# The out projection of a streaming encoder block as 2x2x2 block products by seven products instead of eight

## The chip, the cores and the metric

The kernel runs on one core of a Trainium2 chip. The metric is the device time in microseconds of one execution. Three runs of the kernel before gave 970.71, 971.36 and 972.44 us; the median is 971.36.

## The reference

One encoder layer on 512 tokens (and 16 meta tokens in front), model width 1024, all in fp32. The change concerns `merged @ w_out`; the lines after it are what waits for its result.

```python
xn = rmsnorm(h, norm_mix_g[l])
proj = xn @ w_in[l]
...
y_sb = o_sb @ w_br_sb[l]
y_df = o_df @ w_br_df[l]
gates = jax.nn.sigmoid(xn @ w_gate[l] + b_gate[l]).reshape(B, L_pad, 2, D)
merged = gates[:, :, 0] * y_sb + gates[:, :, 1] * y_df
h = h + merged @ w_out[l]
hn = rmsnorm(h, norm_ffn_g[l])
h = h + (jax.nn.silu(hn @ w_ffn_gate[l]) * (hn @ w_ffn_up[l])) @ w_ffn_down[l]
```

`o_sb` comes from a stick-breaking attention of 8 heads, `o_df` from a differential attention of 8 heads.

## The kernel before

Every matmul is made in three passes (`mm3`, L262 to L264): each operand is split into a rounded high part and the rest (`split`, L76: ScalarE casts the high part, L77; VectorE subtracts it, L78), and high x high, high x low and low x high are summed in PSUM. So everything that TensorE reads, weights too, passes once through ScalarE and VectorE.

The work runs in stages: input projection and the stick-breaking heads, the differential heads, the gate stage, the out projection, the FFN's gate and up projections, the down projection. Activations lie transposed in the gate stage (`mg_h`, `mg_l`: model row by token), so that in the out projection a token tile of 128 is the stationary operand and 512 output columns stream.

**Weights.** All of them form one list, `stream`. `stage_one` (L157) issues the DMA of the next one on SP (L179) into one of three `wst` buffers of 512 KB; `prepare` casts it into one of four `wh`/`wl` pairs. `weights(key)` asks for a chunk and prepares `READY` = 3 (after the first part of the kernel 2) chunks beyond it. A cast can only start when an earlier chunk's pair has been read for the last time.

**Background jobs.** The down projection is already made with seven products instead of eight. Its weight sums are made in DRAM by 48 DMAs on POOL's queue (`sum_job`, L136 to L141): copies of a block, and accumulating ones that read a block and add it to a sum (`ds` in the profile). During the heads one job is put in for every two units of projection work (L993 to L995). Each job waits for the last cast that was written before it, which paces it.

**Gate stage (L1028 to L1038).** For each of the eight 128-row blocks f, both branches' outputs come back from DRAM (`y_back`, `y_part`; stored on POOL's queue at L766 and L768, `y_df<-y_out`), two gates are computed (24 matmuls of 128x512 each; f = 0 and 1 already in the heads' stage), POOL multiplies each gate with its branch (L1036), VectorE adds the two (L1037), and `split` cuts the sum into `mg_h[:, f]`, `mg_l[:, f]`. The residual input `hres` is then loaded by four DMAs on POOL's queue (L1044); the tile takes the place of `y_out`.

**Out projection (`accumulate`, L1047).** Two column halves, each over 8 k and 4 token tiles; half 0 accumulates in the two `z` tiles, half 1 in four `mm` tiles with its last six k token tile by token tile, so that tiles end one after the other. After each tile: VectorE adds the bank into `hres` (L1068), ScalarE squares it with a row sum (L1071), and `done(t)` calls `normed(t)` (rstd, then `hn`, L1092). After tile 2, `turned(0)` transposes tiles 0 and 1 on TensorE (L1101, 16 transposes) and cuts them into `hT_h` (ScalarE, L1106) and `hT_l` (VectorE, L1107). The first FFN products on tokens 0 to 255 follow, then tile 3, `turned(1)`, and `block_sums` (L1113 to L1125), which makes the token sums t1 to t4 that the FFN's seven products need.

The scheduler places instructions on each engine by priorities; each engine then runs its own list in order.

Of the kernel before, what the change touches and what calls it, by code (L numbers as in the profile page):

```python
# [40 lines left out]
def block_kernel(ctx: ExitStack, tc: tile.TileContext, x, meta, norm_mix_g, w_in, w_gate, b_gate,  # L41
# [94 lines left out]
    def sum_job(to, of, k0, add):  # L136
        src = raw_down(of, k0) if of in raw_at else w_sum[of, k0][:, 0:min(2, NK - k0)]
        dst = w_sum[to, k0][:, 0:min(2, NK - k0)]
        kw = dict(accum_op=ALU.add, max_dma_last_dim=2048) if add else {}
        paced = mybir.DependencyInfo(mybir.DependencyClass.Sync, mybir.DependencyReason.DATA)  # L140
        tc.add_manual_dep(nc.gpsimd.dma_start(dst, src, **kw).ins, cast["last"].ins.name, paced)  # L141

    background = [(to, of, k0, i > 3) for i, (to, of) in enumerate(
        (("s1", "a21"), ("s2", "a11"), ("s3", "a21"), ("s4", "a12"), ("s1", "a22"), ("s3", "a11"), ("s2", "s1"), ("s4", "s2")))
        for k0 in DK]
# [880 lines left out]

    ys = [y_back(f) for f in range(2)]
    for f in range(KT):  # L1028
# [3 lines left out]
        for br, y in enumerate(ys[f]):  # L1032
            if f > 1:
                for u in gate(br, f, sg[br], AF.Sigmoid):
                    u()
            nc.gpsimd.tensor_tensor(sg[br], sg[br], y, op=ALU.mult)  # L1036
        nc.vector.tensor_tensor(sg[0], sg[0], sg[1], op=ALU.add)  # L1037
# [9 lines left out]
    def accumulate(pool, name, act, nk, half, tail, done, banks):  # L1047

        if banks == "z":
            zt = [z_tile() for _ in range(2)]  # L1050
            acc = [zt[t // 2][:, t % 2] for t in range(NQ)]
        else:
            acc = [mm_tile() for _ in range(NQ)]

        def step(k, t):
            ah, al = act(half, k)
            wh, wl = weights((name, half, k // 2 * 2))
            q = slice(t * P, (t + 1) * P)
            mm3(acc[t], [(ah[:, q], al[:, q], wh[:, k % 2], wl[:, k % 2])], k == 0, k == nk - 1)

        cs = slice(half * 512, (half + 1) * 512)
        for k in range(nk - tail):
            for t in range(NQ):
                step(k, t)
        for t in range(NQ):
            for k in range(nk - tail, nk):
                step(k, t)
            nc.vector.tensor_tensor(hres[:, t, cs], hres[:, t, cs], acc[t], op=ALU.add)  # L1068
            sq = pool.tile([P, 512], F32, tag="y_sb", bufs=2, name="sq")
# [350 lines left out]
```

## Time and profile before

| | |
|---|---|
| median of 3 runs | 971.36 us |
| the profiled execution | 970.92 us |
| its span | 969.1 us |
| PE busy | 948.4 us |
| VectorE, ScalarE, POOL busy | 701.2, 588.0, 183.8 us |
| gate stage | 505 to 579 us of the span |
| out projection | 578.92 to 624.44 us |
| entry to the FFN | 625 to 660 us |

The profile shows one execution; times in it are microseconds from the span's start. PE is TensorE's matmuls, DVE VectorE, ACT ScalarE, POOL GpSimd, SPq and POOLq the queues that issue DMAs. A row of a timeline has the start, the length, the engine, the line of the kernel and `out<-in`, and in brackets how long the engine had been idle and what released it. Buffer numbers are left out of names: `z` and `mm` are PSUM tiles, `wst` a staged weight, `wh` and `wl` its two parts, `sg` a gate tile, `ds` the weight sums in DRAM. Matmuls are pipelined, so their lengths overlap; the distance of their starts is what one costs.

### The profile page before, as it was taken

To read this page: it belongs to the slowest core of one execution; us is meant where nothing else is said; L and a number is where in the kernel's file an instruction comes from. 1 tells how busy PE (TensorE), PEld (TensorE's weight loads), DVE (VectorE), ACT (ScalarE), POOL (GpSimd) and SP (SyncE) were. 2 spreads that over 40 slices of the span, in tenths; PEclk is the share of its full clock that TensorE was granted. 3 is DMA by queue.
4 is the path that set the end of the run, shared out by engine and by line. 5 is a ranking of instruction groups with operands and counts; after the bars stand their busy time and mean duration, and the time that the engine had idled before them with its cause. 6 is when DMAs were issued, how large, how long until landed. Compare 5 with 4: busy or idle time off the path is not lost.

```text
span 969.1 us, 16156 instructions
## 1 busy us (share of the span) xinstructions
PE 948.4 (98%) x6117; PEld 853.8 (88%) x6118; DVE 701.2 (72%) x1292; ACT 588.0 (61%) x1128; POOL 183.8 (19%) x198
## 2 busy tenths in 40 slices
PE   8998999999999999999999999989999999999997
PEld 6997888898899998999878888879999999988886
DVE  7988687766567776678632433699888888989785
ACT  7666766666566666666773433575555555666554
POOL 3201111222353433422315430000000000000013
PEclk9999999999999999999999999999999999999999
DMA  8334656679989989754739733124433334276552
GB/s 242 109 104 126 188 167 176 171 164 208 194 183 189 172 199 198 155 139 111 153 100 259 237 121 100 57 62 134 129 89 111 108 95 123 67 240 205 181 168 87
DMA packets 151439, 145.83 MB, mean 150 GB/s; under 512 B 6049, under 2 KB 116802, under 8 KB 151362
## 3 DMA queue, kind: packets, MB, share of 16 engines
q1 hardware_dynamic: 131794, 97.94, 34.0%
q0 software_dynamic: 19408, 46.80, 23.8%
q8 instruction: 48, 0.79, 0.3%
q14 instruction: 29, 0.24, 0.1%
q10 hardware_dynamic: 160, 0.07, 0.0%
HBM read 121.59 MB, written 41.94 MB: 169 GB/s over the span
## 4 chain that ended last, share of the span: by engine, by line
PE 86%; DVE 6%; ACT 4%; DMA 3%; issue 1%; DVEq 0%; ACTq 0%; SPq 0%
PE mm L264 19%; PE mm L263 19%; PE mm L262 19%; PE z L262 7%; PE z L263 7%; PE z L264 7%; DMA wst<-in_w_in_dram 2%; PE z L673 1%; PE z L672 1%; DVE wl L78 1%; PE tr L528 1%; PE z L528 1%; ACT wh L77 1%; PE tr L504 1%; PE z L556 0%
## 5 line engine op out<-in xcount | busy, mean ns | idle before, releaser
L262 PE MATMUL mm<-xT_h,wh 128*128 128x264 f32 (+2 forms) x656 | 214.3, 327 | 0.5 <-ACT xT_h L865 0.5
L78 DVE TENSOR_TENSOR wl<-wst,wh 128x1024 fp32r<-128x1024 f32 (+1 forms) x146 | 162.3, 1116 | 72.1 <-ACT wh L77 72.0
L263 PE MATMUL mm<-xT_l,wh 128*128 128x264 f32 (+2 forms) x656 | 213.2, 325 | 0.5
L264 PE MATMUL mm<-xT_h,wl 128*128 128x264 f32 (+2 forms) x656 | 212.8, 324 | 0.0
L77 ACT CAST wh<-wst 128x1024 fp32r<-128x1024 f32 (+1 forms) x146 | 140.2, 962 | 103.0 <-PE mm L263 70.0
L263 PEld LDWEIGHTS mm<-xT_l,wh 128*128 128x128 f32 x656 | 123.4, 188 | 10.4 <-DVE xT_l L866 1.3
L262 PEld LDWEIGHTS mm<-xT_h,wh 128*128 128x128 f32 x656 | 123.6, 188 | 10.0 <-ACT xT_h L865 0.9
L264 PEld LDWEIGHTS mm<-xT_h,wl 128*128 128x128 f32 x656 | 123.4, 188 | 9.9
L263 PE MATMUL mm<-hT_l,wh 128*128 128x256 f32 x284 | 80.6, 285 | 0.7 <-DVE hT_l L1107 0.7
L262 PE MATMUL mm<-hT_h,wh 128*128 128x256 f32 x284 | 80.3, 285 | 0.6 <-DVE sg L1202 0.6
L264 PE MATMUL mm<-hT_h,wl 128*128 128x256 f32 x284 | 80.1, 283 | 0.0
L1322 POOL TENSOR_TENSOR outs<-hres,gF 128x512 f32<-128x512 f32 x4 | 7.2, 1799 | 283.2 <-DVE hres L1308 278.1
L141 POOL DMA_DIRECT2D ds<-in_w_ffn_down_dram x36 | 28.5, 791 | 156.0 <-ACT wh L77 106.0
L676 DVE CUSTOM_DVE_ANT_0 pr<-z,bias 128x144 f32<-128x144 f32 (+3 forms) x64 | 30.9, 502 | 35.0 <-PE z L673 34.9
L263 PEld LDWEIGHTS mm<-hT_l,wh 128*128 128x128 f32 x284 | 53.7, 189 | 1.1 <-DVE hT_l L1107 1.1
L262 PEld LDWEIGHTS mm<-hT_h,wh 128*128 128x128 f32 x284 | 53.4, 189 | 1.0 <-DVE sg L1202 0.8
L264 PEld LDWEIGHTS mm<-hT_h,wl 128*128 128x128 f32 x284 | 53.6, 189 | 0.0
L262 PE MATMUL mm<-o_h,wh 128*128 128x512 f32 x128 | 53.1, 415 | 0.0
L262 PE MATMUL z<-wh,da 128*128 128x512 f32 (+1 forms) x132 | 50.9, 386 | 0.3 <-DVE hres L1308 0.3
L264 PE MATMUL mm<-o_h,wl 128*128 128x512 f32 x128 | 50.8, 397 | 0.0
L263 PE MATMUL mm<-o_l,wh 128*128 128x512 f32 x128 | 50.1, 392 | 0.3 <-DVE o_l L744 0.3
L263 PE MATMUL z<-wl,da 128*128 128x512 f32 (+1 forms) x132 | 50.4, 382 | 0.0
(344 smaller groups left out, 2560.1 us busy)
## 6 DMA issues: line engine op xcount, KB each, us to landing
wst<-in_w_in_dram SPq DMA_DIRECT2D x40, 512.0 KB, 7.2
ds<-in_w_ffn_down_dram POOLq DMA_DIRECT2D x30, 512.0 KB, 5.1
wst<-in_w_ffn_gate_dram SPq DMA_DIRECT2D x22, 512.0 KB, 3.8
wsu<-in_w_ffn_up_dram SPq DMA_DIRECT2D x21, 512.0 KB, 3.8
y_df<-y_out POOLq DMA_DIRECT2D x32, 256.0 KB, 5.7
wst<-in_w_gate_dram SPq DMA_DIRECT2D x16, 512.0 KB, 5.9
slots<-ds SPq DMA_DIRECT2D x13, 512.0 KB, 3.3
ds<-ds POOLq DMA_DIRECT2D x10, 512.0 KB, 8.1
```

The costliest lines, as they stand in the source:

```text
L77: cast["last"] = (hi_copy or nc.scalar.copy)(hi, src)
L78: (lo_eng or nc.vector).tensor_tensor(lo, src, hi.bitcast(F32), op=ALU.subtract)
L141: tc.add_manual_dep(nc.gpsimd.dma_start(dst, src, **kw).ins, cast["last"].ins.name, paced)
L262: nc.tensor.matmul(ps, lhsT=ah, rhs=bh, start=(start and i == 0), stop=False, skip_group_check=skip)
L263: nc.tensor.matmul(ps, lhsT=ah, rhs=bl, start=False, stop=False, skip_group_check=skip)
L264: nc.tensor.matmul(ps, lhsT=al, rhs=bh, start=False, stop=(stop and i == n - 1), skip_group_check=skip)
L504: nc.tensor.transpose(pt[:, j * P:(j + 1) * P], vT[:, j * P:(j + 1) * P], ident)
L528: nc.tensor.transpose(pt[:, (t - j) * P:(t - j + 1) * P], blocks(t, j * P, (j + 1) * P), ident)
L672: nc.tensor.matmul(o, lhsT=q[c][:, qs], rhs=k[c][:, 0, k0:k1], start=True, stop=False)
L673: nc.tensor.matmul(o, lhsT=q[c][:, qs], rhs=k[c][:, 1, k0:k1], start=False, stop=True)
L676: nc.vector.tensor_tensor_reduce(po, zz, bb, scale=1.0, scalar=-3.0e38, op0=ALU.add, op1=ALU.max, accum_out=mx[:, t, c:c + 1])
L1322: nc.gpsimd.tensor_tensor(outs[t][:, D1], hres[:, t, D1], gF[:, D1], op=ALU.mult)
```

## The change

`merged` (512 x 1024) and `w_out` (1024 x 1024) are each taken as 2x2 blocks. The product is made with seven block products instead of eight, each of 256 tokens x 512 k x 512 columns, two token tiles and 4 k each:

- The list `OUT` names them: weight operand, token operand, PSUM accumulator. Three accumulators, `acc[0]` to `acc[2]`, each of two banks, are added into `hres` (`to_out`) as soon as a product that completes a term is done: 14 adds of 128x512 instead of 8.
- The weight sums s1 to s4 are made in DRAM by 16 more background jobs, 8 copies and 8 accumulating ones, of two 128x512 blocks each. They stand ahead of the 48 jobs of the down projection. `tick` replaces the count of units; it is also called in the gate stage after each gate unit, and twice per step of the FFN loop.
- The out projection reads 14 weight chunks of 512 KB instead of 8 (six raw, eight sums). Two of every five of them are loaded into the upper half of a new tile `mf` (`oslots`) instead of a `wst` buffer; `READY` is 3 for them.
- The token sums t1 to t4 are made in the gate loop (`merge_sums`). For f below 4 the merged row stays in `mf`; t1 is cut from it. For f from 4 on, t2, t3 and t4 are made of rows f and f - 4. `b12`, the row block that no product uses alone, is not cut; t3 takes its place in `mg_h` and `mg_l`.
- Token tiles 0 and 1 are complete after the fifth product; tiles 2 and 3 after the sixth and seventh, which are made for tile 2 first and then for tile 3.

The diff, cut to its core:

```diff
+    o_sum = {(n, k0): sums_dram.tile([P, 2, 512], F32, name=f"o{n}_{k0}") for n in ("s1", "s2", "s3", "s4") for k0 in (0, 2)}
+    OUT = (("a11", "b11", 0), ("s1", "t1", 2), ("s2", "t2", 0), ("s4", "b22", 2), ("s3", "t3", 0), ("a12", "b21", 1),
+           ("a22", "t4", 0))
...
+    def sum_jobs(raw, kept, ks):
+        return [lambda to=to, of=of, k0=k0, i=i: summed_in(kept(to, k0), (raw if of[0] == "a" else kept)(of, k0), i > 3)
+                for i, (to, of) in enumerate((("s1", "a21"), ("s2", "a11"), ("s3", "a21"), ("s4", "a12"),
+                                              ("s1", "a22"), ("s3", "a11"), ("s2", "s1"), ("s4", "s2")))
+                for k0 in ks]
...
+    background = sum_jobs(raw_out, lambda w, k0: o_sum[w, k0], (0, 2)) + sum_jobs(raw_down, lambda w, k0: w_sum[w, k0][:, 0:min(2, NK - k0)], DK)
+    ticks = [0]
+
+    def tick(num=1, den=2):
+        ticks[0] += 1
+        if background and ticks[0] * num // den > (ticks[0] - 1) * num // den:
+            background.pop(0)()
...
-            slot = (n - first_down) % 7 - 3 if n >= first_down else -1
-            if slot < 0:
+            slot = (n - first_down) % 7 - 3 if n >= first_down else (n - first_out) % 5 - 3 if key[0] == "out" else -1
+            if key[0] == "out" and slot >= 0:
+                st = fpools["oslots"][:, slot]
+            elif slot < 0:
...
+    def merge_sums(f, m):
+        k = f % 4
+        b11, b12 = mf[:, k, T2], mf[:, k, T1]
+        if f < 4:
+            split(mg_h[:, f, T2], mg_l[:, f, T2], b11)
+            nc.vector.tensor_tensor(b11, b11, b12, op=sub)
+            split(*(v[:, k] for v in tsum["t1"]), b11)
+        else:
+            b21, b22 = m[:, T2], m[:, T1]
+            nc.vector.tensor_tensor(b11, b11, b22, op=add)
+            cut(tsum["t2"], k, b11, -1.0)
+            split(mg_h[:, f], mg_l[:, f], m)
+            nc.vector.tensor_tensor(b12, b22, b12, op=sub)
+            split(mg_h[:, k, T1], mg_l[:, k, T1], b12)
+            nc.vector.tensor_tensor(b21, b11, b21, op=sub)
+            split(*(v[:, k] for v in tsum["t4"]), b21)
...
                 for u in gate(br, f, sg[br], AF.Sigmoid):
                     u()
+                    tick()
             nc.gpsimd.tensor_tensor(sg[br], sg[br], y, op=ALU.mult)
-        nc.vector.tensor_tensor(sg[0], sg[0], sg[1], op=ALU.add)
-        split(mg_h[:, f], mg_l[:, f], sg[0])
+        m = mf[:, f] if f < 4 else sg[0]
+        nc.vector.tensor_tensor(m, sg[0], sg[1], op=ALU.add)
+        merge_sums(f, m)
...
-    accumulate(mgp, "out", merged, KT, 0, 0, lambda t: None, "z")
-    accumulate(mgp, "out", merged, KT, 1, 6, done, "mm")
...
+    def out_steps(i, t):
+        w, b, e = OUT[i]
+        ah, al = otok[b]
+        q = slice(t * P, (t + 1) * P)
+        for k in range(4):
+            wh, wl = weights(("out", w, k // 2 * 2))
+            mm3(acc[e][t], [(ah[:, k, q], al[:, k, q], wh[:, k % 2], wl[:, k % 2])],
+                k == 0 and w in ("a11", "s1", "a12"), k == 3, True)
...
+    for t in range(2):
+        out_steps(5, t)
+        to_out(2 + t, 0, acc[1][t], add, True)
+        out_steps(6, t)
+        to_out(2 + t, 1, acc[0][t], sub, True)
```

The scheduler puts the changed program into another order on each engine. Three places matter below.

POOL in the gate stage, before. `y_df<-y_out` are the stores of the differential branch's rows, `sg<-sg,y_sb` and `sg<-sg,y_df` the products of a gate with its branch.

```order
158 L1036 TENSOR_TENSOR sg<-sg,y_sb 128x512 x2
159 L768 DMA y_df_115<-y_out 128x512
160 L768 DMA y_df_116<-y_out 128x512
161 L768 DMA y_df_117<-y_out 128x512
162 L768 DMA y_df_118<-y_out 128x512
163 L1036 TENSOR_TENSOR sg<-sg,y_df 128x512
164 L768 DMA y_df_119<-y_out 128x512
165 L1036 TENSOR_TENSOR sg<-sg,y_df 128x512
166 L768 DMA y_df_120<-y_out 128x512
167 L768 DMA y_df_121<-y_out 128x512
168 L1044 DMA hres<-in_x_dram 128x1024 x2
169 L1036 TENSOR_TENSOR sg<-sg,y_sb 128x512
```

And now, from row 2's store on (`ds<-ds` are accumulating jobs):

```order
172 L791 DMA y_df_124<-y_out 128x512
173 L143 DMA ds_2_103<-ds_2_91 256x512
174 L791 DMA y_df_125<-y_out 128x512
177 L791 DMA y_df_128<-y_out 128x512
178 L1089 TENSOR_TENSOR sg<-sg,y_df 128x512 x2
179 L143 DMA ds_4_104<-ds_4_92 256x512
180 L791 DMA y_df_129<-y_out 128x512
181 L1098 DMA hres<-in_x_dram 128x1024
182 L1089 TENSOR_TENSOR sg<-sg,y_sb 128x512
183 L143 DMA ds_6_105<-ds_6_93 256x512
185 L143 DMA ds_8_106<-ds_8_94 256x512
186 L1089 TENSOR_TENSOR sg<-sg,y_df 128x512
```

(Rows 175, 176 and 184, two more stores and two `hres` loads, are left out.) Jobs of the down projection's sums now stand between the stores, ahead of the last store (`y_df_129`, row 7), and between the products of row 2. Before, none stood here.

TensorE where the out projection ends, before. `z<-ident,hn` are the transposes of `turned(0)`:

```order
3588 L262 MATMUL mm<-wh,mg_h 128x512
3589 L1101 MATMUL z<-ident,hn 128x128 x4
3590 L263 MATMUL mm<-wl,mg_h 128x512
3591 L264 MATMUL mm<-wh,mg_l 128x512
3592 L262 MATMUL mm<-wh,mg_h 128x512
3593 L263 MATMUL mm<-wl,mg_h 128x512
3594 L264 MATMUL mm<-wh,mg_l 128x512
3595 L1101 MATMUL z<-ident,hn 128x128 x4
3596 L262 MATMUL mm<-wh,mg_h 128x512
3597 L263 MATMUL mm<-wl,mg_h 128x512
3598 L264 MATMUL mm<-wh,mg_l 128x512
3599 L262 MATMUL mm<-hT_h,wh 128x256
```

And now, after the last matmul of the out projection and five of the FFN:

```order
3579 L287 MATMUL mm<-hT_h,wl 128x256
3580 L285 MATMUL mm<-hT_h,wh 128x256 x2
3581 L286 MATMUL mm<-hT_l,wh 128x256
3582 L285 MATMUL mm<-hT_h,wh 128x256
3583 L286 MATMUL mm<-hT_l,wh 128x256
3584 L1124 MATMUL z<-ident,hn 128x128 x4
3585 L286 MATMUL mm<-hT_l,wh 128x256
3586 L1124 MATMUL z<-ident,hn 128x128 x4
3587 L287 MATMUL mm<-hT_h,wl 128x256
3588 L286 MATMUL mm<-hT_l,wh 128x256
```

The last eight transposes of `turned(0)` have moved from before the end of the out projection to behind the first twelve matmuls of the FFN.

VectorE at the same place, before. `hn` is the normed tile, `hT_l` the low part of its transpose, `hres` the residual add, `wl` the low part of a weight:

```order
797 L1092 TENSOR_SCALAR hn<-hres,rs 128x1024
798 L1068 TENSOR_TENSOR hres<-hres,mm 128x512
799 L1107 SCALAR_TENSOR_TENSOR hT_l<-z,pcol,hT_h 128x256
800 L347 TENSOR_SCALAR rs<-ssq 128x1
801 L1107 SCALAR_TENSOR_TENSOR hT_l<-z,pcol,hT_h 128x256 x2
802 L357 SCALAR_TENSOR_TENSOR rs<-rs 128x1
803 L353 TENSOR_SCALAR rs<-rs 128x1
804 L355 TENSOR_TENSOR rs<-rs 128x1
805 L1092 TENSOR_SCALAR hn<-hres,rs 128x1024
```

And now:

```order
845 L1115 TENSOR_SCALAR hn<-hres,rs 128x1024
846 L1170 TENSOR_TENSOR hres<-hres,mm 128x512
847 L1130 SCALAR_TENSOR_TENSOR hT_l<-z,pcol,hT_h 128x256
848 L370 TENSOR_SCALAR rs<-ssq 128x1
849 L1130 SCALAR_TENSOR_TENSOR hT_l<-z,pcol,hT_h 128x256
850 L78 TENSOR_TENSOR wl<-wst,wh 128x1024
851 L1170 TENSOR_TENSOR hres<-hres,mm 128x512
852 L78 TENSOR_TENSOR wl<-wst,wh 128x1024
853 L380 SCALAR_TENSOR_TENSOR rs<-rs 128x1
854 L1170 TENSOR_TENSOR hres<-hres,mm 128x512
855 L376 TENSOR_SCALAR rs<-rs 128x1
856 L1130 SCALAR_TENSOR_TENSOR hT_l<-z,pcol,hT_h 128x256
```

Between the second and the third cut of `turned(0)` there now stand two residual adds and two weight casts.

More of the change, by code (lines that the diff above doesn't have):

```diff
@@ L134, in raw_down, with raw_out @@
         return w_fd[:, k + k0:k + min(k0 + 2, NK), c0:c0 + 512]
[L136 to L145, printed above, removed]
+    def raw_out(w, k0):
+        k, c0 = out_at[w]
+        return w_out[:, k + k0:k + k0 + 2, c0:c0 + 512]
+    background = sum_jobs(raw_out, lambda w, k0: o_sum[w, k0], (0, 2)) + sum_jobs(raw_down, lambda w, k0: w_sum[w, k0][:, 0:min(2, NK - k0)], DK)
[4 more added lines that the diff above has]
+            background.pop(0)()
     at_of = {c[0]: n for n, c in enumerate(stream)}
@@ L149, in block_kernel @@
     first_down = at_of["down", "a11", 0]
+    first_out = at_of["out", "a11", 0]
     staged, loaded = [], {}
@@ L960, in block_kernel @@
     turn()
-    todo, unit_count = [], [0]
+    todo = []
     for br in range(2):
@@ L1045, in block_kernel @@
     ssq = [small.tile([P, 2], F32, tag=f"ssq{t}", bufs=2, name="ssq") for t in range(NQ)]
[L1047 to L1069, printed above, removed]
-            s0, s1 = ssq[t][:, 0:1], ssq[t][:, 1:2]
-            nc.scalar.activation(sq, hres[:, t, cs], AF.Square, accum_out=(s1 if half else s0))
-            if half == 0:
-                nc.vector.tensor_scalar(s0, s0, 1.0 / D, EPS, op0=ALU.mult, op1=ALU.add)
-            done(t)
     hT_h, hT_l = (xtp.tile([P, NM + KT * SEQ], F32R, tag=t, name=n)[:, NM:].rearrange("p (k t) -> p k t", t=SEQ)
@@ L1130, in done, with to_out @@
             turned(0)
-    def merged(half, k):
-        return mg_h[:, k], mg_l[:, k]
-    accumulate(mgp, "out", merged, KT, 0, 0, lambda t: None, "z")
-    accumulate(mgp, "out", merged, KT, 1, 6, done, "mm")
+    e1 = [mm_tile() for _ in range(2)]
+    acc = [[mm_tile() for _ in range(2)], e1, (lambda z: [z[:, 0], z[:, 1]])(z_tile())]
+    def out_steps(i, t):
[6 more added lines that the diff above has]
+                k == 0 and w in ("a11", "s1", "a12"), k == 3, True)
+    def to_out(t, half, ps, op, last=False):
+        cs = slice(half * 512, (half + 1) * 512)
+        with tc.high_priority(offset=EVAC):
+            nc.vector.tensor_tensor(hres[:, t, cs], hres[:, t, cs], ps, op=op)
+        if last:
+            sq = mgp.tile([P, 512], F32, tag="y_sb", bufs=2, name="sq")
+            s0, s1 = ssq[t][:, 0:1], ssq[t][:, 1:2]
+            nc.scalar.activation(sq, hres[:, t, cs], AF.Square, accum_out=(s1 if half else s0))
+            if half == 0:
+                nc.vector.tensor_scalar(s0, s0, 1.0 / D, EPS, op0=ALU.mult, op1=ALU.add)
+            else:
+                done(t)
+    for i in range(5):
+        for t in range(2):
+            out_steps(i, t)
+            ps = acc[OUT[i][2]][t]
+            if i == 0:
+                to_out(2 + t, 0, ps, add)
+            elif i == 1:
+                to_out(t, 1, ps, sub)
+            elif i == 2:
+                to_out(t, 0, ps, add)
+            elif i == 3:
+                to_out(t, 0, ps, add, True)
+            else:
+                to_out(t, 1, ps, sub, True)
+    for t in range(2):
+        out_steps(5, t)
+        to_out(2 + t, 0, acc[1][t], add, True)
+        out_steps(6, t)
+        to_out(2 + t, 1, acc[0][t], sub, True)
     early = [mm_tile(), mm_tile()]
@@ L1279, in block_kernel @@
             ready(at_job(c4, f) + 2)
+            tick(1, 1)
+            tick(1, 1)
+        assert not background
         tp_ctx.close()
```

42 lines of the change are left out of this document (30 added, 12 removed).

## The prediction

> **What bounds the kernel now.** The page comes first: the span, each engine's share of it, and the chain of work that ended last.
>
> ```profile
> span 969.1 us, 16156 instructions
> PE 948.4 (98%) x6117; PEld 853.8 (88%) x6118; DVE 701.2 (72%) x1292; ACT 588.0 (61%) x1128; POOL 183.8 (19%) x198
> PE 86%; DVE 6%; ACT 4%; DMA 3%; issue 1%; DVEq 0%; ACTq 0%; SPq 0%
> ```
>
> TensorE is busy for 948.4 of 969.1 us, so a matmul that isn't issued is time saved unless something else then ends last. The profiled execution took 970.92 us, 1.8 more than its span; the median of three is 971.36. I add my sum to 970.92 and shift the result by the 0.44 between the two. About 0.2% (1.9 us) is what a measurement can tell from no change.
>
> The second view is the table by stage, cut at the stages that the change touches. Its columns are the stretch, its length, the busy time of PE, PEld, DVE, ACT and POOL, the granted clock, the DMA share and GB/s.
>
> ```profile
> 300.00:400.00 100.00, 100.00 (x670) 91.97 (x670) 70.70 (x181) 66.23 (x156) 39.02 (x43) 1.00 0.89 188
> 505.00:579.00 74.00, 74.00 (x328) 61.27 (x327) 25.88 (x27) 28.23 (x40) 33.03 (x27) 1.00 0.75 212
> 579.00:625.00 46.00, 46.00 (x214) 37.97 (x213) 21.68 (x41) 19.49 (x39) 1.75 (x1) 1.00 0.22 69
> 625.00:660.00 35.00, 30.64 (x238) 28.62 (x237) 32.49 (x49) 27.08 (x52) 0.59 (x1) 1.00 0.35 104
> 660.00:860.00 200.00, 200.00 (x1658) 198.96 (x1657) 173.19 (x270) 113.59 (x186) 0.00 (x0) 1.00 0.37 107
> ```
>
> The gate stage (505 to 579) and the out projection (579 to 625) leave PE without a gap. Behind them, 625 to 660, PE idles for 4.4 of 35 us and VectorE is busy for 32.49: this entry to the FFN is the one place near the change where PE already waits. From 660 PE is full again. So three things count: how many matmuls go, what the entry gives back, and whether the gate stage, where POOL and DMA get more to do, stays full.
>
> **The change: the matmuls.** PE's timeline at the two ends of the out projection (start, length, line, work):
>
> ```profile
> 578.92 0.39 PE L262 MATMUL z<-wh,mg_h 128*128 128x512 f32 x1
> 579.14 0.39 PE L263 MATMUL z<-wl,mg_h 128*128 128x512 f32 x1
> 579.37 0.39 PE L264 MATMUL z<-wh,mg_l 128*128 128x512 f32 x1
> ...
> 618.36 1.03 PE L1101 MATMUL z<-ident,hn 128*128 128x128 f32 x8
> ...
> 624.21 0.39 PE L264 MATMUL mm<-wh,mg_l 128*128 128x512 f32 x1
> 624.44 0.28 PE L262 MATMUL mm<-hT_h,wh 128*128 128x256 f32 x1
> ```
>
> The lengths overlap; the pitch counts: three starts, 0.45 us over two steps, and over the whole run 0.2267. Before: 2 halves x 8 k x 4 token tiles x 3 = 192 matmuls, 192 x 0.2267 = 43.5 of the 45.5 us from 578.92 to 624.44; the rest is 16 transposes. After: 7 products x 4 k x 2 token tiles x 3 = 168, of the same 128x512 shape. So 24 x 0.2267 = **-5.44 us**, if PE is fed as well as now. The Trainium skill, "TensorE: Matmul & The Clock Gate", section "Back-to-back issue gap", gives about 131 ns per matmul of 512 columns in a sustained stream with weight loads, and about 216 ns for one alone; by the 131 the saving would be 3.1 us, by the 216 5.2. The trace doesn't agree with the 131: its sustained pitch is 226.7, near to the figure for one alone, and it decides.
>
> **The out projection itself.** Rows by form in 579 to 625 (busy, mean ns of one | idle before), and the table load ahead of the first square:
>
> ```profile
> L77 ACT CAST wh<-wst 128x1024 fp32r<-128x1024 f32 x9 | 9.5, 1052 | 14.7 <-PE z L264 4.4 <-issue 3.9 <-PE mm L263 3.8
> L78 DVE TENSOR_TENSOR wl<-wst,wh 128x1024 fp32r<-128x1024 f32 x7 | 8.6, 1224 | 17.2 <-ACT wh L77 17.2
> L1068 DVE TENSOR_TENSOR hres<-hres,mm 128x512 f32<-128x512 f32 x3 | 2.1, 688 | 3.0 <-PE mm L264 3.0
> ...
> 583.12 0.62 ACT L77 CAST mg_h<-sg 128x512 fp32r<-128x512 f32 x1 [2.59 <-DVE sg L1037]
> 583.75 1.28 ACT L67 ACT_TABLE_LOAD   x1
> 585.05 1.05 ACT L77 CAST wh<-wst 128x1024 fp32r<-128x1024 f32 x1
> ```
>
> Six more weight chunks cost 6 x 1.05 = 6.3 us of ScalarE and 6 x 1.22 = 7.3 of VectorE; six more residual adds 6 x 0.69 = 4.1 of VectorE; the token sums come in the gate stage, where both engines are busy for under 29 of 74 us. VectorE thus goes from 21.7 us busy in 46 to about 33 in 41: covered, if nothing is late in order. One is. Each product uses two chunks, 24 matmuls or 5.4 us for both. The four chunk buffers are full when the stage begins, so the cast of s2's second chunk waits until a11's 24 matmuls are done. Ahead of it on ScalarE stand the last row's cuts and the 1.28 us table load, which came at 583.75 before, when the following cast had nothing to hurry for. Stepping through the order with these durations, that chunk's low part is ready 10.9 us after the stage begins, and s2 asks for it at about 10: **+1.0** (bounds 0, if the cuts are done before the stage begins, and +2.3, cast plus load all in the open).
>
> **The entry to the FFN.** VectorE's string there, and PE's waits between 505 and 660:
>
> ```profile
> 613.13 0.76 DVE L1092 TENSOR_SCALAR hn<-hres,rs 128x1024 f32<-128x1024 f32 x1
> 617.16 0.75 DVE L1092 TENSOR_SCALAR hn<-hres,rs 128x1024 f32<-128x1024 f32 x1
> ...
> 625.43 0.68 DVE L1068 TENSOR_TENSOR hres<-hres,mm 128x512 f32<-128x512 f32 x1
> ...
> 648.76 1.22 DVE L1122 SCALAR_TENSOR_TENSOR t_l<-bf,t_h 128x1024 fp32r<-128x1024 f32 x1
> ...
> PE mm L263 <- DVE t_l L1122: 1.1, 1, 1.1
> PE mm L262 <- ACT wh L77: 0.9, 1, 0.9
> PE mm L263 <- DVE hT_l L1107: 0.7, 2, 0.4
> PE mm L262 <- DVE sg L1202: 0.6, 1, 0.6
> ```
>
> PE waits for t_l, the sum t2 that the FFN's products need, and 24.5 us lie from the last residual add to the end of that step (625.43 to 649.98). Before, all 16 transposes of the first half were through before the out projection ended. Now (the rows of PE's order, shown with the change) the second eight come behind twelve matmuls of the FFN, and VectorE's order has two residual adds and two weight casts among the first half's cuts. So the first matmuls on `hT` find only half of it cut: each half takes four ScalarE and four VectorE cuts of 0.48 us, and two adds (1.4 us) stand among them. I take **+1.3**, the two adds; bounds are 0 (all of it lies beside other matmuls) and 3.8 (two adds and two 1.22 us casts, all in the open). Ahead of the first eight transposes, `hn` of the second tile follows a12's first add on VectorE: **+0.45** (0 to 0.76, one `hn`). In return the later waits for a cast and for q (0.9 and under) shrink when the weights have had more time: **-0.3** (0 to -1.2).
>
> **The gate stage.** Three groups of rows: POOL, then the releases that set the next gate's weights, then DMA from 505 to 545 (its fortieths, its queues).
>
> ```profile
> 517.08 1.28 POOL L1036 TENSOR_TENSOR sg<-sg,y_df 128x512 f32<-128x512 f32 x1 [4.36 <-DMA y_df<-y_df]
> 521.66 1.76 POOL L768 DMA_DIRECT2D y_df<-y_out  x2
> 528.94 1.12 POOL L1044 DMA_DIRECT2D hres<-in_x_dram  x2 [5.51 <-DMA y_df<-y_out]
> 532.44 1.31 POOL L1036 TENSOR_TENSOR sg<-sg,y_df 128x512 f32<-128x512 f32 x1
> ...
> 536.12 1.23 DVE L78 TENSOR_TENSOR wl<-wst,wh 128x1024 fp32r<-128x1024 f32 x1 [0.26 <-ACT wh L77]
> ...
> 545.60 0.39 PE L262 MATMUL mm<-xT_h,wh 128*128 128x512 f32 x1
> ...
> DMA  8549999999999999969999999999999999989949
> q1 hardware_dynamic: 8491, 6.50, 54.0%
> q0 software_dynamic: 1728, 4.20, 45.9%
> ...
> L141 POOL DMA_DIRECT2D ds<-ds x12: 891/938/1206, 308.2 to 392.8; - x12
> ds<-ds POOLq DMA_DIRECT2D x10, 512.0 KB, 8.1
> ```
>
> The chain is: branch outputs to DRAM and back, POOL's product (532.44), VectorE's sum, the cut of row 2 on ScalarE, and behind that in ScalarE's queue the cast of the next gate's weights. Those are ready at 537.35 (536.12 + 1.23), and PE takes them up at 545.60: **8.2 us of slack**. The 16 new sum jobs come first in the background list, so the 12 accumulating jobs, before all issued from 308 to 393, end later: five of them now stand in POOL's queue between the y_df stores and the products. One stands ahead of the store of row 7, on which POOL's `hres` load waits (5.51 us before); two stand between `hres` and the product of row 2. DMA has no room in these 40 us: 99.9% of its time is taken. A job's accumulation took 8.1 us to land beside such traffic. As throughput, q0 moved 4.20 MB in 45.9% of 40 us, which is 4.4 us per MB, so 2.3 for a job's 0.5 MB. The delay of row 2's sum is then: one or two jobs' traffic ahead (2.3 to 4.6), the late row-7 store (2.3 to 8.1), two to four issues at 0.94 (1.9 to 3.8). End to end that is 6.5 to 16.5, but these overlap in part: 7 to 12, against 8.2 of slack. What is over stalls PE one for one. The low end lies below the slack and the middle 1.3 above it: I take half of that, **+0.6**, with 0 and 8.3 as the ends. The Trainium skill, "DMA: Bandwidth & Descriptors", on arbitration between queues, says that all issuing engines share the same 16 DMA engines and interleave, so the jobs slow the weight loads too; the trace agrees: q0 and q1 together take 99.9% here. This speaks against the change.
>
> The rest costs nothing: in the attention stages PE has 100.00 of 100 busy from 300 to 400 while the DMA share is 0.89 and the same kind of job runs; the eight plain and eight accumulating jobs there (16 issues of 0.7 to 0.94 us on a POOL that is 39% busy) are put at 0, with 1 us either way.
>
> **Sum:** -5.44 + 1.0 + 1.3 + 0.45 - 0.3 + 0.6 = **-2.4**. From 970.92 that is 968.5, by the median 969.0.
>
> **The rivals.**
> *Full gain.* The adds and casts are covered, s2's chunk is in time, the gate stage absorbs all within its 8.2 us. For it: VectorE is busy for only 47% of 579 to 625. Against it: the entry already makes PE wait. Then -5.44 + 0 to 1 of give-back: 966.0 to 967.0, 966.5 in the middle. Chance 0.17.
>
> *Eaten at the entry.* The FFN's first products wait for t2, whose time is set by VectorE's and ScalarE's string and not by when the out projection ends. VectorE is busy for 93% of 625 to 660; the two adds and two casts now in the string are 3.8 us, and with the 1.0 in s2 and 0.45 that makes 5.25 of 5.44. Time about 971.2, no change. Chance 0.28.
>
> *Slower through the gate stage.* The five accumulating jobs hold up the row-7 store, with it `hres`, and with it the product of row 2. It decides from 8.2 us of delay on. Two jobs ahead that land one behind the other (2 x 8.1 = 16.2, the slow end of the rows) make a stall of 8.0; with the -3.0 that is left elsewhere, +5.0: 976.4. With a delay of 14 it is +2.8: 974.2. For it: DMA at 99.9%, and the 5.51 us that POOL waits for that store already. Against: 8.2 us of slack and weights loaded ahead. Chance 0.20.
>
> That the change does not do what it says is excluded: PE's order has 24 rows of 128x512 fewer, 168 in the stage.
>
> **How the numbers follow.** Forecast (partial gain, -1.9 to -4) 0.35, full gain 0.17, eaten 0.28, slower 0.20. Faster by over 0.2%: 0.35 + 0.17 = 0.52; within: 0.28; slower: 0.20. The range: below, 966.0 is -5.4 with nothing given back; above, 973.5, a stall of 5.1 in the gate stage with the -3.0 elsewhere, leaves out most of the slower case. The forecast's own range is 967.4 to 969.5.
>
> **What would show it.** In the profile after: the out projection's matmuls at a pitch of 0.2267 with 168 of them, 38.1 us plus its waits, and a wait of PE for a `wl` in its third product, of about 1 us; waits of PE for `hT_l` or `hn` in the ten microseconds after it that sum to 1 to 2 more than before; in the gate stage PE's first wait, if any, at the weights of the gate of row 5, on an ACT cast behind row 2's cut. It is wrong if the gate stage shows over 4 us of wait, if the entry's waits don't grow, or if the attention stages before 505 are longer or shorter by over 1 us.

## The result and the profile after

| | before | changed |
|---|---|---|
| median | 971.18 us (4 runs) | 984.00 us (982.70 to 986.01, 4 runs) |
| ratio | 1 | 1.0132, interval 1.0112 to 1.0152 |
| the profiled execution / its span | 970.92 / 969.1 | 982.70 / 980.9 |

The change makes the kernel 12.8 us slower. The page of the changed kernel, first the span, the engines and the chain of work that ended last:

```profile
span 980.9 us, 16230 instructions
PE 949.2 (97%) x6093; PEld 851.6 (87%) x6094; DVE 725.8 (74%) x1336; ACT 597.8 (61%) x1150; POOL 198.8 (20%) x214
PE 77%; DVE 8%; issue 6%; ACT 5%; POOL 3%; DMA 1%; SPq 0%; DVEq 0%; POOLq 0%; ACTq 0%
```

PE issues 24 instructions fewer, and is busy for 949.2 us as before (948.4). So some of what is left must run slower. The table by stage, cut at the same events as before (end of the gate stage, end of the out projection):

```profile
505.00:587.50 82.50, 76.83 (x328) 62.07 (x327) 34.08 (x45) 28.37 (x47) 36.19 (x31) 0.98 0.85 213
587.50:635.00 47.50, 43.26 (x178) 33.46 (x177) 35.67 (x59) 27.70 (x49) 4.26 (x3) 0.93 0.39 123
635.00:670.00 35.00, 30.32 (x236) 28.35 (x235) 32.70 (x55) 27.96 (x55) 0.60 (x1) 1.00 0.33 97
```

The first stretch holds the same 328 matmuls as before in 82.5 us instead of 74. In both of the first two PE has idle time, and the granted clock is below 1: 0.98 and 0.93. The waits of PE and the rows where they end (the changed kernel):

```profile
PE mm L287 <- DVE wl L78: 3.1, 1, 3.1
PE mm L285 <- ACT sg L798: 2.6, 1, 2.6
PE mm L285 <- ACT wh L77: 2.3, 1, 2.3
```

```profile
530.32 0.39 PE L286 MATMUL mm<-xT_l,wh 128*128 128x512 f32 x1
533.77 0.51 PE L287 MATMUL mm<-xT_h,wl 128*128 128x512 f32 x1 [3.06 <-DVE wl L78]
...
534.80 0.63 PE L287 MATMUL mm<-xT_h,wl 128*128 128x512 f32 x1
535.23 0.63 PE L285 MATMUL mm<-xT_h,wh 128*128 128x512 f32 x1
...
559.59 0.51 PE L285 MATMUL mm<-xT_h,wh 128*128 128x512 f32 x1 [2.60 <-ACT sg L798]
...
587.57 0.39 PE L285 MATMUL mm<-wh,mg_h 128*128 128x512 f32 x1
...
599.62 0.80 PE L285 MATMUL mm<-wh,t_h 128*128 128x512 f32 x1 [2.34 <-ACT wh L77]
601.55 0.80 PE L286 MATMUL mm<-wl,t_h 128*128 128x512 f32 x1 [1.14 <-DVE wl L78]
...
635.03 0.28 PE L285 MATMUL mm<-hT_h,wh 128*128 128x256 f32 x1
```

Read the starts, not the waits alone. Behind the first wait the matmuls come every 0.43 us (534.80, 535.23) instead of every 0.2267. The clock has been halved:

```profile
531.00:534.00 3.00, 0.23 (x1) 0.23 (x2) 3.00 (x6) 0.81 (x2) 1.87 (x3) 1.00 0.84 210
534.00:538.00 4.00, 4.00 (x12) 3.10 (x11) 3.01 (x7) 3.52 (x6) 0.00 (x0) 0.57 1.09 188
538.00:542.00 4.00, 4.00 (x19) 3.33 (x18) 1.01 (x1) 0.34 (x1) 2.93 (x4) 1.00 0.69 202
...
599.00:606.00 7.00, 5.24 (x11) 3.35 (x12) 5.59 (x10) 3.63 (x5) 0.00 (x0) 0.51 0.29 90
```

Twelve matmuls fall into the four microseconds after the wait, 19 into the next four. Read in steps of 0.1 us, the granted clock is 0.50 from 534.3 to 537.7 and from 599.2 to 606.0, which are stretches of 3.4 and 6.8 us. The Trainium skill, "TensorE: Matmul & The Clock Gate", Part 1 (the HAM clock gate), says that the clock is halved when the array has been idle for a window of about 3.4 us, that the window runs freely, and that it takes about as long to come back. The trace agrees with the length, once and twice 3.4 us; it does not agree that a whole window must be idle, for the waits were 3.06 and 2.34 us.

With the first matmuls of three events as marks (gate stage from the first gate matmul, 513.64 before and 513.77 after; the out projection from its first matmul to the first on `hT`; the entry to the FFN from there to the end of the wait for t_l, 650.03 and 662.46), this is where the time went:

| | before | changed | difference |
|---|---|---|---|
| gate stage | 65.28 | 73.80 | +8.52 |
| out projection | 45.52 | 47.46 | +1.94 |
| entry to the FFN | 25.59 | 27.43 | +1.84 |

The gate stage's +8.52 is the two waits (gaps of 3.45 and 3.00 where 0.23 is normal: 3.22 + 2.77 = 6.0) and 2.5 for matmuls at a lower clock or restarting behind a wait.

What is late there? POOL, VectorE, SP and ScalarE in the changed kernel, to be read beside the rows of before in the prediction:

```profile
504.06 0.90 POOL L143 DMA_DIRECT2D ds<-ds  x1 [24.93 <-ACT wh L77]
510.51 1.54 POOL L143 DMA_DIRECT2D ds<-ds  x1
528.56 2.53 POOL L1089 TENSOR_TENSOR sg<-sg,y_df 128x512 f32<-128x512 f32 x2 [12.95 <-DMA y_df<-y_df]
...
532.51 1.21 DVE L78 TENSOR_TENSOR wl<-wst,wh 128x1024 fp32r<-128x1024 f32 x1
...
541.39 1.33 SPq L202 DMA_DIRECT2D wst<-in_w_gate_dram  x2
...
557.90 1.04 ACT L77 CAST wh<-wst 128x1024 fp32r<-128x1024 f32 x1 [9.64 <-DMA wst<-in_w_gate_dram]
558.85 0.68 ACT L798 ACTIVATE sg<-mm,pcol 128x512 f32<-128x512 f32 x1
```

VectorE's cast of the first chunk, before:

```profile
522.96 1.22 DVE L78 TENSOR_TENSOR wl<-wst,wh 128x1024 fp32r<-128x1024 f32 x1
```

The product of row 0 waits for its load until 528.56; before, it began at 517.08. Two jobs were issued ahead of it, at 504.06 and 510.51. Before, VectorE went on from it to the low part of the weights of the gate of row 3 in time, at 522.96; now that cast begins at 532.51 and PE has been waiting for it since 530.55.

The second wait ends at 559.59 with ScalarE's evacuation of a PSUM bank (558.85). This stands behind a cast of gate weights, which waited 9.64 us for their load. The loads of gate weights that were not yet cast then had been issued at 541.39 (two) and at 553.74. The last one takes 8.5 us to land, until 562.2, and the second of the two takes 18.0 us, until about 560: both come after the cast began at 557.90. That leaves the first of the two, some 16.5 us under way, with jobs issued beside it at 540.88, 542.62 and 547.69. (SP also spends 8.35 us in issuing the load of a branch row at 545.29, where most take 0.32 to 0.34. What it issued afterwards came later for it, but the weights of this wait were issued before.)

DMA between 505 and 560 in the changed kernel (last column: median us to landing):

```profile
wst<-in_w_gate_dram SPq DMA_DIRECT2D x6, 512.0 KB, 14.0
y_df<-y_out POOLq DMA_DIRECT2D x8, 256.0 KB, 10.7
ds<-ds POOLq DMA_DIRECT2D x4, 512.0 KB, 9.2
y_df<-y_df SPq DMA_DIRECT2D x5, 256.0 KB, 13.6
```

and before, between 505 and 545:

```profile
wst<-in_w_gate_dram SPq DMA_DIRECT2D x7, 512.0 KB, 6.0
y_df<-y_out POOLq DMA_DIRECT2D x8, 256.0 KB, 5.8
y_df<-y_df SPq DMA_DIRECT2D x6, 256.0 KB, 4.7
```

The same load of a branch row takes 13.6 instead of 4.7 us, with the jobs beside it (over the same 505 to 560 the kernel before has 4.4 for it, and 6.0 and 5.8 for the other two). That is the theory to test. Its rivals: the jobs' places in POOL's queue, and the token sums' additional work on ScalarE and VectorE.

### The profile page after: what moved, and what is told of

Same layout as the page of the kernel before. It is cut to its first block, busy times and chain, and to the rows that moved or that the text cites. A ratio compares the mean times of both kernels' runs of the same rounds, so it can differ in the third digit from the quotient of the medians.

```text
span 980.9 us, 16230 instructions
## 1 busy us (share of the span) xinstructions
PE 949.2 (97%) x6093; PEld 851.6 (87%) x6094; DVE 725.8 (74%) x1336; ACT 597.8 (61%) x1150; POOL 198.8 (20%) x214
## 4 chain that ended last, share of the span: by engine, by line
PE 77%; DVE 8%; issue 6%; ACT 5%; POOL 3%; DMA 1%; SPq 0%; DVEq 0%; POOLq 0%; ACTq 0%
PE mm L286 17%; PE mm L287 17%; PE mm L285 17%; PE z L285 6%; PE z L286 6%; PE z L287 6%; POOL sg L1089 2%; DVE wl L78 1%; PE z L696 1%; PE z L695 1%; ACT wh L77 1%; PE z L551 1%; PE tr L551 1%; PE tr L527 1%; DMA wsu<-in_w_ffn_up_dram 1%
## 5 line engine op out<-in xcount | busy, mean ns | idle before, releaser
L78 DVE TENSOR_TENSOR wl<-wst,wh 128x1024 fp32r<-128x1024 f32 (+1 forms) x147 | 165.8, 1131 | 59.4 <-ACT wh L77 59.3
```

Source lines behind the costliest of these rows:

```text
L78: (lo_eng or nc.vector).tensor_tensor(lo, src, hi.bitcast(F32), op=ALU.subtract)
```

## The experiments

All comparisons are with the kernel before on the same chip, run beside it; its median there was 972.2 to 972.9 us. The marks of the table above, for every run (us, from PE's timeline):

| run | median | ratio, interval | gate | out | entry |
|---|---|---|---|---|---|
| e1_no_gate_jobs | 977.94 | 1.0053, 1.0035 to 1.0071 | 65.28 | 41.00 | 27.69 |
| e2_before_with_jobs | 982.73 | 1.0105, 1.0088 to 1.0122 | 75.09 | 45.53 | 25.50 |
| e3_thin_gate_jobs | 969.22 | 0.9969, 0.9957 to 0.9981 | 65.28 | 40.98 | 27.36 |
| e4_jobs_early | 976.78 | 1.0054, 1.0035 to 1.0073 | 65.28 | 41.00 | 27.62 |
| e5_jobs_late_ffn | 969.93 | 0.9969, 0.9959 to 0.9979 | 65.28 | 41.01 | 27.49 |
| e6_jobs_gate_tail | 969.77 | 0.9971, 0.9958 to 0.9984 | 65.28 | 40.96 | 27.50 |
| e7_table_later | 969.21 | 0.9970, 0.9960 to 0.9980 | 65.28 | 41.11 | 27.52 |
| e8_product_major | 970.00 | 0.9977, 0.9966 to 0.9988 | 65.28 | 41.79 | 27.87 |
| e9_adds_behind_cuts | 970.35 | 0.9979, 0.9968 to 0.9990 | 65.28 | 41.39 | 26.02 |
| e10_two_z_tiles | 966.84 | 0.9944, 0.9929 to 0.9960 | 65.28 | 39.56 | 27.16 |
| e11_z_and_table | 966.87 | 0.9948, 0.9933 to 0.9962 | 65.28 | 39.54 | 27.55 |
| e12_two_gate_jobs | 974.47 | 1.0022, 1.0008 to 1.0035 | 68.72 | 41.17 | 27.35 |

### Are the jobs of the gate stage the cause?

e1 takes them out of the gate loop (they follow in the FFN loop):

```diff
                 for u in gate(br, f, sg[br], AF.Sigmoid):
                     u()
-                    tick()
```

> The changed kernel without background jobs in the gate stage: its six last accumulating jobs are issued in the FFN loop. Compared with the changed kernel's gate stage (513.8 to 587.6 us, 8.5 longer than before) and out stage (47.5 us instead of 40). Theory traffic (the jobs' bytes delay the y_df loads and all later waits follow) and theory queue (the jobs' places in POOL's order do it): gate stage back to 65.3 us, the stall in the third product down to 1 to 2 us, time 967 to 971 us. Theory cuts (the token sums' work on ScalarE and VectorE makes each row of the gate loop longer, jobs or not): the gate stage stays over 70 us, the time over 978.

Gate stage 65.28 us, as before to the hundredth, and out stage 41.00. So the token sums' cuts cost the gate stage nothing. But the time missed its forecast: 977.94. The jobs have only moved their collision: gate weights of the FFN take 9.6 us to land between 645 and 675 (4.0 in e5, below, which has no jobs there). PE in the FFN loop of e1:

```profile
673.68 0.58 PE L285 MATMUL mm<-hT_h,wh 128*128 128x256 f32 x1 [5.74 <-ACT qx L1271]
```

and POOL in e1, the six jobs two by two:

```profile
651.63 1.89 POOL L143 DMA_DIRECT2D ds<-ds  x2
660.35 1.77 POOL L143 DMA_DIRECT2D ds<-ds  x2 [6.82 <-ACT qy L1276]
674.87 1.71 POOL L143 DMA_DIRECT2D ds<-ds  x2 [12.75 <-ACT wh L77]
```

e2 is the other half of the test: the kernel before, with its eight products, and only the 16 additional jobs and the new pacing.

```diff
+    background = [(out_job, (to, of, k0, i > 3)) for i, (to, of) in enumerate(ALLJ) for k0 in (0, 2)] + [(sum_job, j) for j in background]
...
                 for u in gate(br, f, sg[br], AF.Sigmoid):
                     u()
+                    tick()
```

> The kernel before with its eight-product out projection, and only the 16 additional DRAM sum jobs and the changed kernel's pacing of all 64 jobs (the additional sums are not used by anything). Traffic and queue: gate stage 7 to 9 us longer than before, time 978 to 981. Cuts: gate stage as before within 1 us, time 971 to 973.

Gate stage 75.09, 9.8 us more than before and a little over the 7 to 9 expected, with the same two waits, 2.0 for a `wl` and 3.7 for the same evacuation. Behind each the clock is 0.50 for 3.4 us (from 534.3 and from 561.6):

```profile
PE mm L284 <- ACT sg L797: 3.7, 1, 3.7
PE mm L286 <- DVE wl L78: 2.0, 1, 2.0
```

The jobs alone, without any of the new arithmetic, make the loss. The out projection of before is not hurt by the late rows (45.53): it needs row 7 only in its last k.

### Bytes or places in the queue?

e3 keeps each job's place and wait on POOL, and a sixteenth of its bytes (`thin` is set for the gate loop alone; one of the down projection's sums is left incomplete by it).

```diff
+        if thin:
+            dst, src = dst[:, :, 0:32], src[:, :, 0:32]
```

> The changed kernel in which the six jobs of the gate stage keep their places and waits on POOL but move only 32 of 512 columns, a sixteenth of the bytes (the down projection's sum s4 is left incomplete). Traffic: the gate stage within 1.5 us of that without jobs, time 967 to 972. Queue: as the changed kernel, gate stage over 71 us, time over 979. Cuts: over 978 as well.

Gate stage 65.28, median 969.22. The issues and waits in POOL's order cost nothing; the bytes do. DMA between 505 and 545 in e3: the jobs still land in 5.3 us, and the branch rows' load is back near its 4.7:

```profile
y_df<-y_df SPq DMA_DIRECT2D x5, 256.0 KB, 5.4
ds<-ds POOLq DMA_DIRECT2D x5, 32.0 KB, 5.3
```

e12 leaves the first two jobs at full size where they were, and puts the other four late in the FFN.

```diff
                     u()
-                    tick()
+                    if f == 2:
+                        tick()
```

> The changed kernel with only the first two of the gate stage's jobs left in their places (ahead of the store of row 0 and before that of row 3); the other four go to the FFN, one per step from the seventh step on. If each of the two stalls of the changed kernel's gate stage (3.1 us at 533.8, 2.6 us at 559.6) comes from the jobs just ahead of it: the first stall stays with its half clock, the second goes, gate stage 69 to 71.5 us. If the second only follows from the lateness of the first rows: both stay, gate stage 73 us or more. If it takes four jobs to delay the rows beyond their slack: no stall, 65.3 us.

The first wait stays and the second goes. The gate stage is 68.72 us, just under the 69 to 71.5 expected. So the first wait comes from the two jobs at 504 and 511, and rows that are late by them do not make the second without the later jobs. This run shows something more. Its wait is as long as the changed kernel's (3.15 us), and no half clock follows:

```profile
531.00:534.50 3.50, 0.35 (x2) 0.19 (x2) 3.50 (x5) 0.81 (x2) 1.43 (x2) 1.00 0.77 162
534.50:538.50 4.00, 4.00 (x18) 3.30 (x18) 3.00 (x7) 3.49 (x6) 1.14 (x3) 1.00 0.79 187
```

18 matmuls in the four microseconds after it, where the changed kernel had 12. So a wait of about 3.1 us either costs itself alone (68.72 - 65.28 = 3.44) or some 1.7 us more (11 matmuls from 533.77 to 538.00 take 4.23 instead of 2.49). That fits a window that runs freely, as the Trainium skill, "TensorE: Matmul & The Clock Gate", Part 1, has it. The changed kernel's own stretches at half clock fit it too: they last 3.4 and 6.8 us, and the 61.5 us between them (537.7 to 599.2) are about 18 times 3.4.

### Where can the jobs go?

```diff
-def tick(num=1, den=2):
+def tick(num=2, den=3):
```

> The changed kernel with two jobs for every three units of work instead of one for every two, so that all 64 are issued in the heads, by about 400 us, where the kernel before issued its last. Traffic and queue: gate stage 65.3 us and time as without jobs in the gate stage, 967 to 971, if the heads' stage takes the faster pace without a wait (513.8 us to its end); if not, the heads grow by what is lost. Cuts: over 978.

The gate stage is clean, but it begins at 521.11 instead of 513.64. The heads do not take the faster pace: in the first 100 us PE has one wait of 3.9 us for `o_l` (0.9 before), and the clock is 0.50 in two stretches around it (84.3 to 87.7 and 94.6 to 98.0).

```profile
94.24 0.39 PE L285 MATMUL z<-kh,qh 128*128 128x264 f32 x1 [3.87 <-DVE o_l L648]
```

e5 issues the six one per step of the FFN loop, from the seventh step on, and none in the gate loop, as e1; e6 leaves them in the gate stage, but from row 5 on.

```diff
-            tick(1, 1)
-            tick(1, 1)
+            if f > 5:
+                tick(1, 1)
```

> The changed kernel without jobs in the gate stage; the six last ones are issued one per step of the FFN loop from the seventh step on, instead of two per step from the first as in the run without gate jobs. If that run's 5.7 us wait for a cast at 673.7 us came from six jobs' traffic beside the first FFN weights, it goes: gate stage 65.3 us, out stage 41, no wait over 1.5 us from 660 to 860, time 3 to 4 us below before. If the wait has another cause (the FFN's order), it stays and the time is 3 us or more above before.

```diff
                     u()
-                    tick()
+                    if f > 4:
+                        tick()
```

> The changed kernel with the gate stage's jobs only from row 5 on, where before had a DMA share of 0.35 after 560 us. If only the traffic beside the branch rows' return (510 to 545 us) hurts: gate stage 65.3 us, time 2 to 4 us below before. If any job in this stage hurts, because it delays the out projection's weights too: a wait for a cast of over 2 us in the out stage, time at or above before.

e6 lies within what was expected and e5 at its edge: 0.9969 and 0.9971, about 2.5 to 3 us faster than before. In e5 the 5.7 us wait of e1 is gone, so the jobs made it; that it was their bytes there too, as the landing times say, no run tested by itself. From row 5 on, the same six jobs in the same stage cost nothing.

The reason is not that DMA has room in e6. On POOL its jobs are issued from 540.28 to 564.56, the first three (540.28, 546.35, 550.05) at nearly the times of the changed kernel's last three. Between 540 and 570 the DMA share of e6 is 1.06, where before has 0.56, and the loads beside the jobs are slower too: 8.4 us for a branch row and 8.1 for gate weights, against 4.4 and 4.5 in e1 without jobs. But PE waits for none of them. So the second wait of the changed kernel needs the late rows (or the jobs' closer spacing) as well as the jobs; no run here separates these two.

### What keeps the rest of the saving?

In e6 the out stage is 4.56 us shorter than before and the entry 1.91 longer. PE's largest waits in e6 behind the gate stage:

```profile
PE mm L286 <- DVE t_l L1146: 1.2, 1, 1.2
PE mm L286 <- DVE hT_l L1131: 0.9, 2, 0.5
PE mm L285 <- ACT hT_h L1130: 0.9, 1, 0.9
PE mm L286 <- DVE wl L78: 0.8, 1, 0.8
PE z L1125 <- DVE hn L1116: 0.6, 1, 0.6
```

The wait for `wl` is the one at s2's second chunk that the prediction spoke of. e7 (on e5) moves the table load behind that cast:

```diff
-    use_table(LN_EXP)
...
     for i in range(5):
+        if i == 3:
+            use_table(LN_EXP)
```

> The late-FFN variant with the table load for the norm moved behind the casts of the second product's chunk. The 1.0 us stall in the third product (a wait for a wl at 590.5 us of the run without gate jobs) should go if the load makes that cast late: out stage 40.0 us instead of 41.0, time 1 us less than the late-FFN variant. If the buffer's release is what is late, the stall stays within 0.2 us.

The wait for `wl` is gone, the stage is not shorter: another wait has taken its place, on a `z` tile. e7's PE and VectorE:

```profile
591.11 0.50 PE L285 MATMUL z<-wh,t_h 128*128 128x512 f32 x1 [1.03 <-DVE hres L1168]
```

```profile
590.38 0.68 DVE L1168 TENSOR_TENSOR hres<-hres,z 128x512 f32<-128x512 f32 x1
```

s1's two token tiles have the two banks of one `z` tile. Token tile 1 writes its own bank, but may not begin until VectorE has drained tile 0's, and VectorE is behind with casts and cuts. The scheduler knew that, and put three quarters of s2's first token tile ahead of s1's second one, which is why s2's second chunk was wanted 12 matmuls early. e10 (on e6) gives each its own tile, e11 does that and moves the load.

```diff
-    acc = [[mm_tile() for _ in range(2)], e1, (lambda z: [z[:, 0], z[:, 1]])(z_tile())]
+    acc = [[mm_tile() for _ in range(2)], e1, [z_tile()[:, 0] for _ in range(2)]]
```

> The gate-tail variant with the accumulator of s1 and s4 in two z tiles of which one bank each is used, instead of the two banks of one tile. In the run with the later table load PE waited 1.0 us for VectorE's add out of bank 0 before it could write bank 1 of the same tile. With the table load where it was, the stall at the wl of s2's second chunk (0.75 us) should stay, or shrink by the 24 matmuls of s1 that can now run ahead of it: out stage 40.0 to 41.0 us.

> Both: two z tiles and the later table load. If the shared tile is what took the later load's gain, no wait over 0.3 us is left in the first 20 us of the out stage, out stage 39.8 to 40.0 us, time 1 us less than the gate-tail variant. If another wait takes its place again, the out stage stays at 41.

Out stage 39.56 and 39.54, below the 40.0 to 41.0 and 39.8 to 40.0 expected, and no two starts of PE over 0.5 us apart in its first 30 us in either. The wait for `wl` that was expected to stay in e10 is gone as well: with two tiles the table load doesn't matter. e10 is 966.84 us, 0.9944 of before: the fastest version here. Its stages:

```profile
505.00:579.00 74.00, 74.00 (x328) 61.29 (x327) 34.34 (x54) 31.54 (x53) 35.84 (x33) 1.00 0.95 246
579.00:619.00 40.00, 40.00 (x181) 32.73 (x180) 30.81 (x52) 25.05 (x44) 1.75 (x1) 1.00 0.41 133
619.00:654.00 35.00, 30.59 (x240) 28.65 (x239) 32.90 (x54) 28.03 (x55) 0.61 (x1) 1.00 0.33 98
```

Two runs asked about the entry. e8 (on e5) makes the last two products one after the other for both token tiles; e9 (on e6) takes the priority from the residual adds of the last two products, so that VectorE has them behind the cuts.

```diff
         to_out(2 + t, 0, acc[1][t], add, True)
+    for t in range(2):
         out_steps(6, t)
```

> The late-FFN variant with the last two products made product by product for both token tiles, so that a12's chunks are free 24 matmuls earlier. If the entry to the FFN is 2.1 us longer than before because the held chunks make the first FFN casts late, it shrinks to 25.6 us, time 1 to 2 us less. If VectorE's string of adds and cuts sets it, the entry stays 27.5 us or more and the time is the same or worse, since tile 2 ends 12 matmuls (2.7 us) later.

```diff
-        with tc.high_priority(offset=EVAC):
+        with tc.high_priority(offset=ahead):
...
-        to_out(2 + t, 0, acc[1][t], add, True)
+        to_out(2 + t, 0, acc[1][t], add, True, 0)
         out_steps(6, t)
-        to_out(2 + t, 1, acc[0][t], sub, True)
+        to_out(2 + t, 1, acc[0][t], sub, True, 0)
```

> The gate-tail variant (jobs from row 5 on) in which the residual adds of the last two products have no priority, so that VectorE's order has them behind the first half's cuts. If the two adds among the cuts cost the entry its 1.3 us (27.5 instead of 25.6 us from the first matmul on hT to the wait for t_l), the wait for hT_h at the entry goes and the entry shrinks by about 1.3, time 1 us less than the gate-tail variant. If VectorE's total work between hn and t2 sets it, the adds only move and the wait for t_l grows by what is saved ahead of it: same time within 0.5 us.

e8's entry is not shorter, 27.87 us. But it holds 3.4 us at half clock (635.1 to 638.5, behind a wait of 1.24 at 634.07) which e5's has not, so e8 doesn't settle whether the held chunks cost anything.

e9's entry is shorter, 26.02, by 1.5 us, a little more than the 1.3 forecast, and 0.4 of it is lost in the out stage, where four transposes now stand. The waits for the low parts of the sums are 0.75 and 0.5 instead of one of 1.2, neither gone nor grown. Yet the time is 970.35, no better than e6's 969.77. Behind t_l PE waits again, 0.60 for a copy (`qx`) and 0.96 for a cast, and then the clock is halved. e9, and below it e6:

```profile
652.00:655.40 3.40, 3.40 (x18) 3.28 (x17) 2.28 (x4) 1.73 (x3) 0.00 (x0) 0.50 0.89 229
...
652.00:656.00 4.00, 4.00 (x34) 3.80 (x33) 3.69 (x6) 2.25 (x4) 0.00 (x0) 1.00 0.71 230
```

At e6's rate the 18 matmuls would take 2.1 us instead of 3.4, so 1.3 us are lost. So the adds among the cuts do cost the entry 1.3 to 1.5 us. Why moving them behind doesn't shorten the kernel is seen in the profiled execution alone: VectorE is busy for over 32 of the 35 us there (32.49 before, 32.70 in the changed kernel, 32.90 in e10), what is put off comes back as a wait, and the clock goes with it.

## Why the prediction was wrong

**The step that failed** is the gate stage's term, +0.6 where the trace has +8.52, and with it "What is over stalls PE one for one". Three things were wrong in it.

*The wrong row.* It followed the accumulating jobs to the late store of row 7, `hres` and the product of row 2, with 8.2 us of slack. The jobs were felt earlier, in the loads of rows 0 and 1, whose product came 11.5 us late (528.56 against 517.08). The chunk behind them was ready at 524.18 before (522.96 + 1.22), and PE asks for it at about 530.5: a slack of some 6.4 us, which the prediction never worked out. 11.5 is over that, whatever the delay further down would have been: the cast began 9.55 us late (532.51 against 522.96), and 9.55 - 6.4 is the wait of 3.1.

*The price of traffic.* It took 2.3 us for a job's 0.5 MB, as throughput, and 8.1 at the slow end for the job's own landing. The cost fell on others: a 256 KB load went from 4.7 to 13.6 us, and the gate weights from 6.0 to 14.0. Between 505 and 530 the DMA engines are full in both kernels (a share of 1.02 and 1.03), and move 242 GB/s before and 219 with the jobs. Being full was read as contention that costs a little more; it could not be read as a price at all. e3 isolates this: same queue, same waits, a sixteenth of the bytes, no loss. So the 1.9 to 3.8 us that the prediction took for the jobs' issues were no part of it either.

*The clock.* Waits were priced one for one. In the changed kernel the clock is at 0.57 and 0.51 behind those of 3.06 and 2.34 us, which costs some 1.7 us in the gate stage; behind the one of 2.60 it is at 1.00. Neither the sum nor the rival had this.

**What followed from it** is the out stage: 47.46 instead of the 41.0 to 41.8 of e1 and e3 to e9, none of which loses time in the gate stage (e12, which loses 3.44 there, has 41.17). The late rows had not caught up by row 7, the cuts of t2 came late, and PE waited 2.3 and 1.1 us in s2 at a clock of 0.51. That the sums of the last row are wanted in the third product, some 36 matmuls into the stage, makes this out projection sensitive to a late row where the old one was not (45.53 in e2): that dependence was in the order, but was not weighed.

**The rest of the sum held.** Without the gate stage's jobs the forecast was -5.44 + 1.0 + 1.3 + 0.45 - 0.3 = -3.0; e5 and e6 show -2.5 and -2.6 in their medians, -3.0 and -2.8 by their ratios. By the marks of e6 the out stage gives 4.56 (the forecast's terms make 5.44 - 1.0) and the entry takes 1.91 (1.3 + 0.45 - 0.3 = 1.45). The 24 matmuls went at the pitch that was used. The stall at s2 measured 1.03 in e6 (a gap of 1.26 where 0.23 is normal), as forecast. Its reason was only half right: the table load is one of two things that make it, and without the load the shared `z` tile makes the same stall (e7). The wait at the entry for `hT_h`, 0.9, and e9's 1.5 bear out the 1.3. The wait for `hn` came, 0.6, but at the third and fourth tile's transposes and not at the first's. The wait for a cast, 0.9 before, is gone, as the -0.3 had it.

**The attention stages** were put at 0: the gate stage begins at 513.77 instead of 513.64, and between 513.8 and 515.1 in the other runs of the same pace, so that is about right at one job per two units. At two per three it isn't (e4).

**The rivals.** The "slower through the gate stage" rival, given 0.20, is what happened in kind: the five jobs, in that place, over the slack. Its chain was another one than it named, and its 976.4 was 7.6 us short, by the clock and the out stage.

What stays open: on what slack e6's jobs live at a full DMA; and why SP's single load at 545.29 took 8.35 us to issue. In e12, without the four later jobs, the same row's load is issued in 0.34 us, so it hangs on them; what it waits for no run here took apart.

## What to carry to other kernels

Where DMA is already busy all the time, price added background traffic by what it does to the landing times of the loads that others wait for, and look at the first such load and not only at the longest chain; then put the jobs where the loads beside them have slack (here some 35 us later, at no cost, though DMA was full there too). Price a wait of TensorE of about 2 us or more with the matmuls of the next 3.4 us, or 6.8, at half clock as the bad case: it came behind waits of 1.97 (e2), 2.34 and 3.06 us, and not behind 2.60 and 3.15. And where two accumulators share a tile, one that is drained holds back the other: two tiles gave more than any reordering tried here.

## What the runs showed of the hardware

- A wait of 3.06 us was followed by matmuls at a pitch of 0.43 us (granted clock 0.57 over four microseconds), one of 3.15 us in another run by the full pitch. The half clock came in stretches of 3.4 us (changed kernel, e2, e4, e8, e9) or 6.8 us (changed kernel, e1), in e9 behind waits of no more than 0.96 us. After 5.74 us the FFN's 256-column matmuls came every 0.21 us instead of 0.12.
- Accumulating DRAM-to-DRAM jobs of 512 KB about double the landing time of others, or more: 4.7 to 13.6, 6.0 to 14.0 and 5.8 to 10.7 us with five of them in 55 us (one of 256 KB), and in e6 4.4 to 8.4 and 4.5 to 8.1. With the DMA engines full in both (505 to 530), they moved 219 instead of 242 GB/s.
